# A ReLU-and-sum kernel: two row blocks of 111 and 17 rows per partition in place of three of 1, 111 and 16

## The chip, the cores and the metric

The kernel runs on one core of a Trainium2 chip. A core has several engines that work at the same time and wait for one another through semaphores. Three of them matter here: VectorE (DVE in the profile), ScalarE (ACT) and SyncE (SP), which in this kernel only issues DMAs. The data lie in the chip's HBM; DMA engines bring them into the on-chip memory, SBUF, which has 128 partitions. The metric is the time of one execution on the device in microseconds (us), given as a median of several runs.

## The reference

```
batch, seq, dim = 32, 512, 1024
x: float32 [32, 512, 1024]
relu_x = np.maximum(x, 0)
return np.sum(relu_x, axis=-1).astype(np.float32)      # [32, 512]
```

There are 16,384 rows of 1024 values. Of each row the negative values are set to zero and the rest is summed. The input has 67.1 MB and the output 64 KB.

## The kernel before, in words

**Tiling.** Each of the 128 partitions works on 128 rows. The rows of x are cut into three regions (`REGIONS = [1, 111, 16]`, the rows per partition). In a region of n rows per partition, partition p holds the n neighbouring rows from p * n on. So region 0 is one contiguous run of 128 rows; in region 1 the rows of neighbouring partitions are 111 rows (444 KB) apart, and in region 2 they are 16 rows (64 KB) apart. `res` holds the 128 sums of each partition, one column per row, in the order in which the rows come in.

**Chunks.** `buf` has three buffers of 16 rows per partition. Seven chunks of 16 rows go round them (`CHUNKS`). Chunk 0 is made of two DMAs, one row of region 0 and then 15 rows of region 1; chunks 1 to 6 are 16 rows of region 1 each. Behind them comes the tail, all of region 2, in pieces of 8, 4 and 2 rows (`TAIL`), and then the last two rows in four parts by columns: `first` (columns 0 to 911 of the first of them), `second` (columns 400 to 1023 of the last one), `third` (its columns 224 to 399), and the part across the border of the two rows (the last 112 columns of the one and the first 224 of the other), which goes to a tile of its own, `seam`.

**Who issues what.** All DMAs are issued by SP, in program order. The two of chunk 0 are moved to the very front of the program. Before chunk c (c at least 3) SP waits at line 90 until DVE has finished the reduces of chunk c-3, whose buffer is taken over; the same wait stands before the tail, for chunk 4. The tail's pieces are issued at line 104, the column parts at line 115, the seam at line 118. After that SP waits for a transposed tile and stores it (lines 119 to 122), waits for the end of chunk 6 on both engines and for the landing of `third` (lines 123 to 125), stores the 111 columns of region 1 (line 126), and at the end stores the last region (line 224) once both engines have finished (`s_last`). Lines 225 and 226 wait for the stores to land.

**Who computes what.** For chunks 0 to 5, ACT applies the ReLU in place in steps of several rows (line 154, `ACT_STEPS`), and DVE sums these rows with a reduce (line 169, `DVE_STEPS`); each reduce adds one to `s_dve`. In chunk 5, four rows are left out of the steps and done one by one, two on each engine. Such a single row is one instruction on either engine, ReLU and sum together (`on_act` and `on_dve`, lines 130 and 133), and is followed by a short instruction that reads the accumulator. Chunk 6 is done in this manner by both engines: even rows on DVE, odd rows on ACT (lines 185 to 188). In the tail's pieces the rows are counted from the start of the piece: even offsets go to DVE, odd ones to ACT (lines 193 to 198). The last two rows are shared out by columns (lines 200 to 220), and their part sums are collected in `seam` and summed last.

**The first region's way out.** Region 0 has one sum per partition, in column 0 of `res`. After chunk 1, DVE transposes columns 0 to 31 of `res` in blocks of 32 x 32 (line 178), so that the sums of region 0 lie along four partitions, and SP stores four runs of 128 bytes.

Of the kernel before, what the change touches and what calls it, by code (L numbers as in the profile page):

```python
# [3 lines left out]
P = 128  # L4
D = 1024
BIG = 16
NB = 3
REGIONS = [1, 111, 16]
CHUNKS = [[(0, 0, 1), (1, 0, 15)]] + [[(1, 16 * c + 15, 16)] for c in range(6)]
ACT_STEPS = [[16], [7, 9], [7, 9], [7, 9], [4, 5, 7], [3, 4, 5]]  # L10
DVE_STEPS = [[16], [7, 4, 5], [7, 4, 5], [7, 4, 5], [4, 5, 7], [3, 4, 5]]
TAIL = [8, 4, 2]
CUT = 912
HEAD = 224
MID = 400
# [3 lines left out]
def bass_relu_sum_kernel(  # L19
# [14 lines left out]
    fp32 = mybir.dt.float32  # L34
# [4 lines left out]
    B, S, _ = x.shape  # L39
    J = B * S // P  # L40
    NBIG = len(CHUNKS)
    assert BIG * NBIG + sum(TAIL) + 2 == J == sum(REGIONS)

    xr = x.rearrange("b s d -> (b s) d")
    of = out.rearrange("b s -> (b s)")
    start = [sum(REGIONS[:i]) for i in range(len(REGIONS))]
    xv = [
        xr[P * s : P * (s + n), :].rearrange("(p j) d -> p j d", p=P)
        for s, n in zip(start, REGIONS)
    ]  # L50
    ov = [of[P * s : P * (s + n)].rearrange("(p j) -> p j", p=P) for s, n in zip(start, REGIONS)]

    buf = nc.alloc_sbuf_tensor("buf", [P, NB, BIG, D], fp32)
    w = D - CUT
    seam = nc.alloc_sbuf_tensor("seam", [P, 2 + w + HEAD + 3], fp32)
    res = nc.alloc_sbuf_tensor("res", [P, J], fp32)
    turned = nc.alloc_sbuf_tensor("turned", [P, 32], fp32)
    aside = nc.alloc_psum_tensor("aside", [P, 4 * D], fp32)

    n_in = NBIG + len(TAIL) + 3  # L60
    s_in = [nc.alloc_semaphore(f"s_in{i}") for i in range(n_in)]
    s_act = nc.alloc_semaphore("s_act")
    s_dve = nc.alloc_semaphore("s_dve")
    s_fact = nc.alloc_semaphore("s_fact")
    s_fdve = nc.alloc_semaphore("s_fdve")
    s_half = nc.alloc_semaphore("s_half")
    s_seam = nc.alloc_semaphore("s_seam")
    s_last = nc.alloc_semaphore("s_last")
    s_turn = nc.alloc_semaphore("s_turn")
    s_store = nc.alloc_semaphore("s_store")  # L70
    s_out = nc.alloc_semaphore("s_out")

    sp, act, dve = nc.sync, nc.scalar, nc.vector

    NTWO = len(ACT_STEPS)
    done = [sum(map(len, DVE_STEPS[: c + 1])) for c in range(NTWO)]


    tb = NBIG % NB


    code = nc.main_func.blocks[0].instructions
# [5 lines left out]
    for c in range(NBIG + 1):  # L88
        if c >= NB:
            sp.wait_ge(s_dve, done[c - NB])  # L90
        if c < NBIG:
            i = 0
            for g, j, n in CHUNKS[c]:
                sp.dma_start(  # L94
                    out=buf[:, c % NB, i : i + n, :], in_=xv[g][:, j : j + n, :]
# [5 lines left out]
    r = 0  # L101
    tail = []
    for i, n in enumerate(TAIL):
        sp.dma_start(out=buf[:, tb, r : r + n, :], in_=xv[-1][:, r : r + n, :]).then_inc(  # L104
            s_in[NBIG + i], 16
        )
        tail.append((r, n, s_in[NBIG + i]))
        r += n


    rows = xv[-1].rearrange("p j d -> p (j d)")[:, r * D : (r + 2) * D]
    flat = buf[:, tb, r : r + 2, :].rearrange("p j d -> p (j d)")
    first, second, third = [(0, CUT), (D + MID, 2 * D), (D + HEAD, D + MID)]
    for k, (lo, hi) in enumerate((first, second, third)):
        sp.dma_start(out=flat[:, lo:hi], in_=rows[:, lo:hi]).then_inc(  # L115
            s_in[NBIG + len(TAIL) + k], 16
        )
    sp.dma_start(out=seam[:, 2 : 2 + w + HEAD], in_=rows[:, CUT : D + HEAD]).then_inc(s_seam, 16)
    sp.wait_ge(s_turn, 1)
    sp.dma_start(  # L120
        out=of[0:P].rearrange("(k q) -> k q", q=32), in_=turned[0:P:32, 0:32]
    ).then_inc(s_store, 16)
    sp.wait_ge(s_fact, 1)
    sp.wait_ge(s_fdve, 1)
    sp.wait_ge(s_in[-1], 16)
    sp.dma_start(out=ov[1][:, :], in_=res[:, start[1] : start[2]]).then_inc(s_store, 16)


    def on_act(t, acc, to=None):
        return act.activation(t if to is None else to, t, AF.Relu, accum_out=acc)  # L130

    def on_dve(t, acc, to=None):
        return dve.tensor_scalar(  # L133
            out=t if to is None else to,
            in0=t,
            scalar1=0.0,
            scalar2=None,
            op0=ALU.max,
            op1=ALU.add,
            accum_out=acc,  # L140
        )

    def row(c, i):
        return buf[:, c % NB, i, :], res[:, c * BIG + i : c * BIG + i + 1]

    k = 0
    for c in range(NTWO):
        alone = BIG - sum(ACT_STEPS[c])
        act.wait_ge(s_in[c], 16 * len(CHUNKS[c]))
        r = 0  # L150
        ready = []
        for n in ACT_STEPS[c]:
            t = buf[:, c % NB, r : r + n, :]
            act.activation(t, t, AF.Relu).then_inc(s_act, 1)  # L154
            k += 1
            ready += [k] * n
            r += n
        for i in range(BIG - alone // 2, BIG):
            on_act(*row(c, i))
        if alone:  # L160
            dve.wait_ge(s_in[c], 16 * len(CHUNKS[c]))
            for i in range(BIG - alone, BIG - alone // 2):
                on_dve(*row(c, i))
        r = seen = 0
        for n in DVE_STEPS[c]:
            if ready[r + n - 1] > seen:
                seen = ready[r + n - 1]
                dve.wait_ge(s_act, seen)
            dve.tensor_reduce(  # L169
                out=res[:, c * BIG + r : c * BIG + r + n],  # L170
                in_=buf[:, c % NB, r : r + n, :],
                axis=X,
                op=ALU.add,
            ).then_inc(s_dve, 1)
            r += n
        if c == 1:
            dve.wait_ge(s_dve, done[c])
            dve.transpose(out=turned[:, :], in_=res[:, 0:32]).then_inc(s_turn, 1)  # L178


    j0 = NBIG * BIG
    for c in range(NTWO, NBIG):
        act.wait_ge(s_in[c], 16 * len(CHUNKS[c]))
        dve.wait_ge(s_in[c], 16 * len(CHUNKS[c]))
        for i in range(BIG):
            ins = (on_act if i % 2 else on_dve)(*row(c, i))
            if i >= BIG - 2:
                ins.then_inc(s_fact if i % 2 else s_fdve, 1)
    aside_rows = [aside[:, i * D : (i + 1) * D] for i in range(1, 4)]
    for r, n, s in tail:  # L190
        act.wait_ge(s, 16)
        dve.wait_ge(s, 16)
        for i in range(r, r + n):
            t, acc = buf[:, tb, i, :], res[:, j0 + i : j0 + i + 1]
            if (i - r) % 2:
                on_act(t, acc, aside_rows.pop(0) if i >= sum(TAIL) - 5 else None)
            else:
                on_dve(t, acc)
# [6 lines left out]
    k = 2 + w  # L205
# [18 lines left out]
    sp.dma_start(out=ov[-1][:, :], in_=res[:, start[-1] : J]).then_inc(s_out, 16)  # L224
    sp.wait_ge(s_store, 16 * (len(REGIONS) - 1))
    sp.wait_ge(s_out, 16)
# [28 lines left out]
```

## Time and profile before

| What | Value |
|---|---|
| Median of 3 runs | 160.76 us (160.74 to 160.83) |
| The profiled execution, its own time | 160.78 us |
| Its span | 159.4 us |
| DVE busy | 120.7 us, 76% |
| ACT busy | 101.4 us, 64% |
| DMA queue of SP, share of 16 engines' span | 98.0% |
| HBM read, mean rate over the span | 67.11 MB, 421 GB/s |
| One row of 1024 columns on DVE (line 133) | 1216 ns |
| One row of 1024 columns on ACT (line 130, into `buf`) | 1042 ns |
| Reduce of 16 rows on DVE (line 169) | 17221 ns |
| Reduce of 7 rows on DVE (line 169) | 7602 ns |
| Transpose on DVE (line 178) | 213 ns |

The span runs from the first to the last instruction that the hardware profiler saw; the execution's own time is 1.4 us longer. "Busy" counts the instructions of an engine without its waits. A wait is listed as idle time before the instruction that it held up, with an arrow to what ended it. "SPq" is the queue in which SP issues its DMAs; the time to landing counts from the issue until the semaphore is complete. Durations of neighbouring instructions on one engine overlap a little, since the next one starts while the last one drains.

### The profile page before, as it was taken

Reading aid. Unit: us, or ns where it says so; the run is one execution under the profiler, and the core shown is the slowest. Engines: PE = TensorE matmul, PEld = TensorE weight load, DVE = VectorE, ACT = ScalarE, POOL = GpSimd, SP = SyncE. Lnnn points to the kernel's source line nnn. Section 1 sums busy time; section 2 is a strip of 40 time slices with the busy share of each in tenths; the row PEclk is TensorE's granted clock in tenths of the full one; section 3 lists DMA queues with packets and bytes.
Section 4 is the critical chain, followed back from the end, with each engine's and each line's share of the span. In section 5 each row is a group of like instructions: output and inputs, shape, how many; then the busy total and the mean of one; then the engine's idle time right before and its main releaser. Section 6 shows DMA issues by size and latency. Waiting matters only on the chain.

```text
span 159.4 us, 150 instructions
## 1 busy us (share of the span) xinstructions
DVE 120.7 (76%) x59; ACT 101.4 (64%) x54; POOL 0.2 (0%) x4
## 2 busy tenths in 40 slices
DVE  0000000009999999999999999999999999898995
ACT  3000059990799808996099951999329990496975
POOL 0000000000000000000000000000000000000000
DMA  9997996996997998989969969969969979798994
GB/s 378 493 401 339 493 526 263 526 526 263 526 460 329 526 411 378 526 362 428 526 296 493 526 263 526 526 263 526 510 280 526 444 345 526 304 485 366 423 399 146
DMA packets 2457, 67.18 MB, mean 421 GB/s; under 512 B 536, under 2 KB 792, under 8 KB 1176
## 3 DMA queue, kind: packets, MB, share of 16 engines
q1 hardware_dynamic: 2456, 67.18, 98.0%
q14 instruction: 1, 0.01, 0.0%
HBM read 67.11 MB, written 0.07 MB: 421 GB/s over the span
## 4 chain that ended last, share of the span: by engine, by line
DVE 54%; DMA 34%; ACT 9%; SPq 1%; issue 0%
DVE res L169 54%; DMA buf<-in_x_dram 34%; ACT buf L154 9%; SPq L104 1%; SPq L115 0%; DVE seam L133 0%; SPq L94 0%; ACT aside L130 0%; DVE turned L178 0%
## 5 line engine op out<-in xcount | busy, mean ns | idle before, releaser
L169 DVE TENSOR_REDUCE res<-buf 128x4 f32<-128x4096 f32 (+4 forms) x16 | 99.3, 6276 | 35.6 <-ACT buf L154 35.6
L154 ACT ACTIVATE buf<-buf 128x7168 f32<-128x7168 f32 (+5 forms) x13 | 80.4, 6233 | 46.2 <-DMA buf<-in_x_dram 46.2
L133 DVE TENSOR_SCALAR_CACHE_REDUCE buf<-buf 128x1024 f32<-128x1024 f32 (+3 forms) x20 | 20.9, 1100 | 1.6 <-DMA buf<-in_x_dram 1.4
L130 ACT ACTIVATE buf<-buf 128x1024 f32<-128x1024 f32 x14 | 14.6, 1042 | 7.9 <-DMA buf<-in_x_dram 7.9
L130 ACT ACTIVATE aside<-buf 128x1024 f32<-128x1024 f32 (+2 forms) x5 | 4.1, 828 | 1.1 <-DMA buf<-in_x_dram 1.0
L130 ACT ACTIVATION_READ_ACCUMULATOR buf<-buf 128x1 f32 x14 | 2.6, 186 | 0.0
L154 ACT ACT_TABLE_LOAD x1 | 1.3, 1283 | 1.3 <-PEq L240 1.3
L133 DVE DVE_READ_ACCUMULATOR buf<-buf 128x1 f32 x20 | 1.7, 83 | 0.0
L130 ACT ACTIVATION_READ_ACCUMULATOR aside<-buf 128x1 f32 x5 | 0.9, 187 | 0.0
L133 DVE TENSOR_SCALAR_CACHE_REDUCE seam<-seam 128x227 f32<-128x227 f32 x1 | 0.4, 391 | 0.0
L130 ACT ACTIVATE aside<-seam 128x114 f32<-128x114 f32 x1 | 0.3, 270 | 0.0
L178 DVE STREAM_TRANSPOSE turned<-res 128x32 f32<-128x32 f32 x1 | 0.2, 213 | 0.0
L130 ACT ACTIVATION_READ_ACCUMULATOR aside<-seam 128x1 f32 x1 | 0.2, 186 | 0.0
L240 POOL MEMSET const-bfloat16-1.0<- 128x1 bf16 x1 | 0.1, 102 | 0.0
L240 POOL MEMSET const-uint8-127<- 128x1 uint8 x1 | 0.1, 102 | 0.0
L240 POOL MEMSET const-float32-1.0<- 128x1 f32 x1 | 0.1, 99 | 0.0
L240 POOL MEMSET const-float32-0.0<- 128x1 f32 x1 | 0.1, 98 | 0.2 <-issue 0.2
L133 DVE DVE_READ_ACCUMULATOR seam<-seam 128x1 f32 x1 | 0.1, 82 | 0.0
## 6 DMA issues: line engine op xcount, KB each, us to landing
buf<-in_x_dram SPq DMA_DIRECT2D x1, 7680.0 KB, 21.2
buf<-in_x_dram SPq DMA_DIRECT2D x1, 4096.0 KB, 25.5
buf<-in_x_dram SPq DMA_DIRECT2D x1, 2048.0 KB, 30.0
buf<-in_x_dram SPq DMA_DIRECT2D x1, 1024.0 KB, 32.0
buf<-in_x_dram SPq DMA_DIRECT2D x1, 512.0 KB, 3.4
buf<-in_x_dram SPq DMA_DIRECT2D x1, 456.0 KB, 32.6
buf<-in_x_dram SPq DMA_DIRECT2D x1, 312.0 KB, 33.0
seam<-in_x_dram SPq DMA_DIRECT2D x1, 168.0 KB, 32.6
```

The lines of the kernel that those rows point to most:

```text
L104: sp.dma_start(out=buf[:, tb, r : r + n, :], in_=xv[-1][:, r : r + n, :]).then_inc(s_in[NBIG + i], 16)
L130: return act.activation(t if to is None else to, t, AF.Relu, accum_out=acc)
L133: return dve.tensor_scalar(out=t if to is None else to, in0=t, scalar1=0.0, scalar2=None, op0=ALU.max, op1=ALU.add, accum_out=acc,)
L154: act.activation(t, t, AF.Relu).then_inc(s_act, 1)
L169: dve.tensor_reduce(out=res[:, c * BIG + r : c * BIG + r + n], in_=buf[:, c % NB, r : r + n, :], axis=X, op=ALU.add,).then_inc(s_dve, 1)
L178: dve.transpose(out=turned[:, :], in_=res[:, 0:32]).then_inc(s_turn, 1)
L240: nc = _bacc.Bacc("TRN2", target_bir_lowering=False, num_devices=1)
```

## The change

The rows are cut into two regions, of 111 and 17 rows per partition. The first DMA takes one row per partition of the first region, at the region's stride, and the second DMA its next 15 rows; the chunks 1 to 5 are 16 rows and chunk 6 is 15 rows. The tail is the second region: 9, 4 and 2 rows and the last two by columns. It starts in the row of the buffer that chunk 6 leaves free and runs on into the next buffer, through a view `line` of the buffers as one run of rows. Chunk 0 is reduced in two steps, of 7 and 9 rows. In chunk 6, ACT takes the even rows and DVE the odd ones. The transpose, its tile, its semaphore and its store are gone; the first region's store takes columns 0 to 110 of `res`, and the last store has 17 columns.

```
-REGIONS = [1, 111, 16]
-CHUNKS = [[(0, 0, 1), (1, 0, 15)]] + [[(1, 16 * c + 15, 16)] for c in range(6)]
+REGIONS = [111, 17]
+CHUNKS = [[(0, 0, 1), (0, 1, 15)]] + [[(0, 16 * c, 16)] for c in range(1, 6)] + [[(0, 96, 15)]]
 ACT_STEPS = [[16], [7, 9], [7, 9], [7, 9], [4, 5, 7], [3, 4, 5]]
-DVE_STEPS = [[16], [7, 4, 5], [7, 4, 5], [7, 4, 5], [4, 5, 7], [3, 4, 5]]
-TAIL = [8, 4, 2]
+DVE_STEPS = [[7, 9], [7, 4, 5], [7, 4, 5], [7, 4, 5], [4, 5, 7], [3, 4, 5]]
+TAIL = [9, 4, 2]
...
+    j0 = sum(n for c in CHUNKS for _, _, n in c)
...
-    turned = nc.alloc_sbuf_tensor("turned", [P, 32], fp32)
...
-    s_turn = nc.alloc_semaphore("s_turn")
...
-    tb = NBIG % NB
+    line = buf[:, :, :, :].rearrange("p b j d -> p (b j) d")
+    t0 = NBIG % NB * BIG - (BIG - CHUNKS[-1][0][2])
...
     for i, n in enumerate(TAIL):
-        sp.dma_start(out=buf[:, tb, r : r + n, :], in_=xv[-1][:, r : r + n, :]).then_inc(
+        sp.dma_start(out=line[:, t0 + r : t0 + r + n, :], in_=xv[-1][:, r : r + n, :]).then_inc(
             s_in[NBIG + i], 16
         )
...
-    flat = buf[:, tb, r : r + 2, :].rearrange("p j d -> p (j d)")
+    flat = line[:, t0 + r : t0 + r + 2, :].rearrange("p j d -> p (j d)")
...
-    sp.wait_ge(s_turn, 1)
-    sp.dma_start(
-        out=of[0:P].rearrange("(k q) -> k q", q=32), in_=turned[0:P:32, 0:32]
-    ).then_inc(s_store, 16)
     sp.wait_ge(s_fact, 1)
     sp.wait_ge(s_fdve, 1)
     sp.wait_ge(s_in[-1], 16)
-    sp.dma_start(out=ov[1][:, :], in_=res[:, start[1] : start[2]]).then_inc(s_store, 16)
+    sp.dma_start(out=ov[0][:, :], in_=res[:, : start[1]]).then_inc(s_store, 16)
...
-        if c == 1:
-            dve.wait_ge(s_dve, done[c])
-            dve.transpose(out=turned[:, :], in_=res[:, 0:32]).then_inc(s_turn, 1)
-
-    j0 = NBIG * BIG
...
     for c in range(NTWO, NBIG):
+        last = sum(n for _, _, n in CHUNKS[c]) - 1
         act.wait_ge(s_in[c], 16 * len(CHUNKS[c]))
         dve.wait_ge(s_in[c], 16 * len(CHUNKS[c]))
-        for i in range(BIG):
-            ins = (on_act if i % 2 else on_dve)(*row(c, i))
-            if i >= BIG - 2:
-                ins.then_inc(s_fact if i % 2 else s_fdve, 1)
+        for i in range(last + 1):
+            ins = (on_dve if i % 2 else on_act)(*row(c, i))
+            if i >= last - 1:
+                ins.then_inc(s_fdve if i % 2 else s_fact, 1)
...
         for i in range(r, r + n):
-            t, acc = buf[:, tb, i, :], res[:, j0 + i : j0 + i + 1]
+            t, acc = line[:, t0 + i, :], res[:, j0 + i : j0 + i + 1]
             if (i - r) % 2:
                 on_act(t, acc, aside_rows.pop(0) if i >= sum(TAIL) - 5 else None)
             else:
                 on_dve(t, acc)
```

More of the change, by code (lines that the diff above doesn't have):

```diff
@@ L41, in bass_relu_sum_kernel @@
     NBIG = len(CHUNKS)
-    assert BIG * NBIG + sum(TAIL) + 2 == J == sum(REGIONS)
+    j0 = sum(n for c in CHUNKS for _, _, n in c)
+    assert j0 + sum(TAIL) + 2 == J == sum(REGIONS)
     xr = x.rearrange("b s d -> (b s) d")
```

## The prediction, made before the result was known

> **What bounds the kernel now.** I read the page first, for the shares of the engines and of the DMA queue.
>
> ```profile
> span 159.4 us, 150 instructions
> DVE 120.7 (76%) x59; ACT 101.4 (64%) x54; POOL 0.2 (0%) x4
> q1 hardware_dynamic: 2456, 67.18, 98.0%
> ```
>
> The queue that brings x in is busy 98% of the span; VectorE (DVE), busier than ScalarE (ACT), stands at 76%. The kernel is a stream of loads, and the times at which ACT starts each chunk confirm it: chunks 0 to 5 start at 21.70, 41.05, 60.41, 79.76, 99.10 and 118.45 us, every 19.35 us for 16 rows per partition, 1.21 us a row. Before the tail, compute matters only if it holds up an issue on SP. So I went to the end, first in the chain of work that ended last.
>
> ```profile
> 122.04 0.33 SPq L104
> ...
> 123.86 32.98 DMA buf<-in_x_dram
> 156.84 0.02 issue
> 156.86 0.03 ACT aside L130
> 156.88 0.43 issue
> 157.32 0.20 ACT aside L130
> 157.51 0.02 issue
> 157.53 0.40 DVE seam L133 x2
> ```
>
> The tail's loads are issued around 122 to 125 us and land 33 us later: they queue behind chunk 6. After the landing of `second` at 156.86 only 1.1 us of compute is left before the last store. The chain's long run of L169 ahead of this is an issue condition with much slack, not a cost: the tail was issued at 122.04, when the stream still had chunk 6 to move until 137.81.
>
> Third, the order of time from the landing of the tail's first piece (8 rows), for DVE and the store, with the idle time before each instruction in brackets.
>
> ```profile
> 147.53 1.22 DVE L133 TENSOR_SCALAR_CACHE_REDUCE buf<-buf 128x1024 f32<-128x1024 f32 x1 [0.50 <-DMA buf<-in_x_dram]
> ...
> 150.95 1.22 DVE L133 TENSOR_SCALAR_CACHE_REDUCE buf<-buf 128x1024 f32<-128x1024 f32 x1
> ...
> 152.09 0.08 DVE L133 DVE_READ_ACCUMULATOR buf<-buf 128x1 f32 x1
> ...
> 152.42 1.22 DVE L133 TENSOR_SCALAR_CACHE_REDUCE buf<-buf 128x1024 f32<-128x1024 f32 x1 [0.24 <-DMA buf<-in_x_dram]
> ...
> 154.94 1.22 DVE L133 TENSOR_SCALAR_CACHE_REDUCE buf<-buf 128x1024 f32<-128x1024 f32 x1 [0.15 <-DMA buf<-in_x_dram]
> ...
> 156.08 0.62 DVE L133 TENSOR_SCALAR_CACHE_REDUCE buf<-buf 128x456 f32<-128x456 f32 x1
> ...
> 156.86 0.37 DVE L133 TENSOR_SCALAR_CACHE_REDUCE buf<-buf 128x208 f32<-128x208 f32 x1
> ...
> 157.16 0.33 DVE L133 TENSOR_SCALAR_CACHE_REDUCE buf<-buf 128x176 f32<-128x176 f32 x1
> ...
> 157.53 0.39 DVE L133 TENSOR_SCALAR_CACHE_REDUCE seam<-seam 128x227 f32<-128x227 f32 x1
> ...
> 157.96 0.34 SPq L224 DMA_DIRECT2D out_dram<-res  x1
> ```
>
> This list decides the case. DVE does every other row; its starts are 1.14 us apart (150.95 minus 147.53, by 3), since each starts when its predecessor's accumulator read starts. Between the pieces its idle time is only 0.24, 0.15 and, before 156.86, about 0.15 us: some 0.5 us of slack from 147.53 to the end.
>
> **The change part by part.** The profiled execution took 160.78 us for a span of 159.4, and the median of the runs is 160.76. What I add to the span I add to 160.76.
>
> *The tail's first piece, 9 rows for 8.* Chunk 6 is one row shorter, so 120 rows per partition have come in when the piece lands, exactly as before (1+111+8 then, 111+9 now), in as many DMAs: it lands at 147.53 if the start of the stream is unchanged. The tail's loop is untouched and gives DVE the rows with even offset: of 8 rows 4, of 9 rows 5; ACT keeps 4. From 147.53 DVE then has 5+2+1 rows without a gap: 8 x 1.14 = 9.12, to 156.65. The half of `first` (456 columns) takes 0.55 from start to the next accumulator read (156.08 to 156.63): 157.20. That is 0.34 after the landing of `second`, the wait that ended last before. Then 208 columns (0.30, from 156.86 to 157.16): 157.50; 176 columns to its accumulator read (0.25, to 157.41): 157.75; from that read to the seam 0.12 (157.41 to 157.53): 157.87. The seam stood at 157.53. **+0.34 us**. The waits between cost nothing once fulfilled: the one before 156.08 leaves the 1.14 spacing. Behind the late seam stand s_last, SP's last issue (157.96 becomes 158.30) and its store; ACT's last part also waits for DVE's 176 columns and moves as far. The other DMA waits of the tail (4 rows, 2 rows, `first`, `second`, `third`, seam load) are then all over before DVE asks.
>
> *Chunk 6, 15 rows, parity swapped.* It lands one row earlier, at 137.81 - 1.21 = 136.60. ACT takes 8 rows at 1.04 (138.87 to 139.91): 144.9. DVE, still in its reduces until 137.27, takes 7 at 1.14: 145.3. Both are ready for 147.53 with 2.2 us in hand; cost nothing. That slack can't be spent: the ninth row lands with its piece.
>
> *Chunk 0's reduce in two steps (7, 9), the transpose gone.* A 7-row reduce takes 7602 ns and the 16-row one 17221 ns, 1069 ns a row; 7+9 make 17.34, so at most +0.12 on DVE. The transpose and its wait gave the next reduce its start at 70.22 after an end at 70.07: -0.15. SP's issue of chunk 3 moves from 52.84 to at most 52.96, while chunk 2 keeps the queue busy until 60.41; the tail's issue at 122.04 has the same cover until 136.6. Nothing, with over 7 us of slack at each.
>
> *The transposed store.* On SP its 0.64 us issue at 125.34 goes, ahead of a wait that lasts until 157.16; in the rings its 0.5 KB lies behind the seam load. The queue's own waits show whether its landing was ever waited for:
>
> ```profile
> SPq L125 <- DMA buf<-in_x_dram: 31.1, 1, 31.1
> SPq L226 <- DMA out_dram<-res: 1.1, 1, 1.1
> ```
>
> No wait stands at L225 (s_store); only the last store, L226, is waited for. So removing it saves nothing. [...]
>
> *The stores that stay.* The large one keeps 444 bytes per partition and is issued at the landing of `third`, 157.16. The last one has 68 bytes per partition instead of 64. The trace shows packets of the 444-byte store from 158.0 to 158.42 and of the 64-byte one from 158.79 to 159.09: 0.42 and 0.30 us. So 4 bytes more, no longer on 64-byte steps, cost 0 to +0.12; it is far nearer the 64-byte row, and I take **+0.02**.
>
> *The tail's pitch, 17 rows for 16.* Eight rows took 147.53 - 137.81 = 9.72 us against 8 x 1.21 = 9.68 at the stream's pace: 0.04 at most to win, and I take 0. [...]
>
> *The first row, strided.* The first DMA read 512 KB in one run; now it reads 128 pieces of 4 KB, 444 KB apart. No row shows this at the start. Before, it landed 3.4 us after its issue, of which 1.21 are data at the stream's pace. In the DMA records few packets run from about 1.1 to 1.4 us, a hole of 0.3. If the hole goes: -0.3; if another like it comes: +0.3. The floor is the landing of the 8 KB store, 1.4 us, plus 1.21 of data: 2.6 against 3.4, -0.8. The nearest rows are `first`, 128 strided pieces of 3.6 KB, landed 1.1 us behind the 2-row piece against 1.08 by its bytes, and chunk 0's other 15 rows, already 444 KB apart, at 18.25 us against 18.14. They say that stride is harmless, so I take 0. What the start gains or loses goes through whole: it moves 147.53.
>
> Sum: 0.34 + 0.02 = 0.36, **161.12 us**. A measurement of this kernel can tell about 0.2% (0.32 us) from no change, so this lies just past that line.
>
> **The rivals.** *The start is slower:* 0.36 + 0.3 gives 161.42. For it: in the old order the first bytes came from one contiguous run. Against: the 15 strided rows behind lost only 0.1.
>
> *The start is quicker and cancels:* without the hole, 147.53 becomes 147.23 and the end stands at 160.82, within 0.2%. For it: the hole is there. Against: nothing in it points to contiguity.
>
> *Faster:* the start is the only place ahead of 147.53 with time to recover. The first landing must come more than 0.68 us sooner (0.36 to pay back, 0.32 to be seen), at 2.7 after its issue; at the floor of 2.6 the sum is 160.3. Against: all of the latency but 0.1 would have to go.
>
> **How the numbers follow.** DVE's odd row with the start unchanged: 0.62, own range 161.0 to 161.25; the line at 161.08 cuts it, about 0.50 above and 0.12 below. Slower start: 0.12. Quicker start that cancels: 0.17. Faster: 0.09. So slower 0.62, same 0.29, faster 0.09. The range reaches to both start cases, 160.75 to 161.5; what is left out is the faster case and a start that loses more than 0.4.
>
> **What would show it.** Right: five DVE rows from the tail's first landing, no DMA wait on DVE from there to the seam, the seam starting 10.34 us after that landing (10.00 before), and the last issue 0.34 later against it. The landing itself, 147.53 before, reads the start by itself, and the first DMA's 3.4 us says whether the stride did it. Packets of the last store over more than 0.3 us would show the 68 bytes. Wrong: a landing moved by over 0.3, or DVE rows not 1.14 apart.

## The result, and the profile after

The changed kernel takes 161.57 us (median of 6 runs, 161.44 to 162.21); the kernel before, on the same chip, 160.82. The ratio is 1.005, with a 95% interval of 1.0033 to 1.0067: slower, by 0.75 us. The forecast was slower, 161.12, with a range up to 161.5. The direction and one mechanism were right; the size was twice what was forecast, and the time lies 0.07 us above the range.

The profiled execution took 161.55 us for a span of 160.2 (before: 160.78 for 159.4). First the page, its span, its engines and its DMA queue:

```profile
span 160.2 us, 149 instructions
DVE 120.2 (75%) x59; ACT 101.4 (63%) x54; POOL 0.2 (0%) x4
q1 hardware_dynamic: 2448, 67.18, 97.7%
```

The stream is as full as before, and DVE even works half a microsecond less, 0.2 of it the transpose that is gone. None of this says where 0.8 us went. The chain that ended last does (start, duration, what):

```profile
0.42 21.47 DMA buf<-in_x_dram
...
122.10 25.63 DMA buf<-in_x_dram
147.73 0.02 issue
147.75 10.31 DVE buf L129 x22
158.06 0.02 issue
158.09 0.40 DVE seam L129 x2
```

Before, the DMA carried the chain until 156.84. Now it hands over to DVE at 147.75, the landing of the 9-row piece, and DVE carries it to the seam in 22 instructions without a break. In the order of time, from chunk 0 on ACT to the last issue on SP:

```profile
21.92 13.86 ACT L150 ACTIVATE buf<-buf 128x16384 f32<-128x16384 f32 x1 [19.39 <-DMA buf<-in_x_dram]
...
147.75 1.22 DVE L129 TENSOR_SCALAR_CACHE_REDUCE buf<-buf 128x1024 f32<-128x1024 f32 x1 [2.45 <-DMA buf<-in_x_dram]
...
152.32 1.22 DVE L129 TENSOR_SCALAR_CACHE_REDUCE buf<-buf 128x1024 f32<-128x1024 f32 x1
...
156.88 0.62 DVE L129 TENSOR_SCALAR_CACHE_REDUCE buf<-buf 128x456 f32<-128x456 f32 x1
...
157.43 0.36 DVE L129 TENSOR_SCALAR_CACHE_REDUCE buf<-buf 128x208 f32<-128x208 f32 x1
...
158.09 0.39 DVE L129 TENSOR_SCALAR_CACHE_REDUCE seam<-seam 128x227 f32<-128x227 f32 x1
...
158.51 0.34 SPq L217 DMA_DIRECT2D out_dram<-res  x1
```

And from the list of DMA issues, the first load and the last store, with KB and the time from issue to landing:

```profile
buf<-in_x_dram SPq DMA_DIRECT2D x1, 512.0 KB, 3.8
...
out_dram<-res SPq DMA_DIRECT2D x1, 8.5 KB, 1.6
```

Subtract the same moments of the two profiles, and the difference falls into three pieces:

| Stretch | Before | After | Difference |
|---|---|---|---|
| Start to chunk 0 on ACT | 21.70 | 21.92 | +0.22 |
| Chunk 0 to the landing of the tail's first piece | 125.83 | 125.83 | 0 |
| That landing to the seam on DVE | 10.00 | 10.34 | +0.34 |
| Seam to the last issue | 0.43 | 0.42 | 0 |
| Last issue to its landing | 1.4 | 1.6 | +0.2 |

The sum is 0.76, and the profiled executions differ by 0.77. The first DMA landed 3.8 us after its issue instead of 3.4.

### The profile page after: what moved, and what is told of

The parts are those of the page before. It is cut to its first block, busy times and chain, and to the rows that moved or that the text cites. A ratio compares the mean times of both kernels' runs of the same rounds, so it can differ in the third digit from the quotient of the medians.

```text
span 160.2 us, 149 instructions
## 1 busy us (share of the span) xinstructions
DVE 120.2 (75%) x59; ACT 101.4 (63%) x54; POOL 0.2 (0%) x4
## 4 chain that ended last, share of the span: by engine, by line
DVE 61%; DMA 29%; ACT 9%; SPq 0%; issue 0%
DVE res L165 54%; DMA buf<-in_x_dram 29%; ACT buf L150 9%; DVE buf L129 6%; DVE seam L129 0%; SPq L94 0%
## 5 line engine op out<-in xcount | busy, mean ns | idle before, releaser
L165 DVE TENSOR_REDUCE res<-buf 128x7 f32<-128x7168 f32 (+4 forms) x17 | 99.3, 5915 | 35.8 <-ACT buf L150 35.8
```

The costliest lines, as they stand in the source:

```text
L165: dve.tensor_reduce(out=res[:, c * BIG + r : c * BIG + r + n], in_=buf[:, c % NB, r : r + n, :], axis=X, op=ALU.add,).then_inc(s_dve, 1)
```

## The experiments

The theory that the table gives is three separate losses: the strided first read, DVE's fifth row, and the 68-byte store. "Excess" below is a kernel's median less that of the kernel before on the same chip (160.83, 160.82 and 160.81 in the three groups). The changed kernel's excess is 0.75.

### DVE's fifth row

```
-            if (i - r) % 2:
+            if (i - r) % 2 != n % 2:
```

> The changed kernel with one edit: in the tail's 9-row piece ACT takes the even offsets (5 rows) and DVE the odd ones (4). Theory (three separate losses: +0.22 us at the start, +0.34 us from DVE's fifth row, +0.2 us at the last store): the seam starts 10.00 us after the landing of the first tail piece instead of 10.34, DVE waits for DMAs again in the tail, and the time falls by 0.34, to about 161.2. Rival (the tail's end is set by something else, the 17-row pitch of the small loads or SP): the seam stays 10.3 us behind that landing and the time stays at 161.55.

Measured: 161.67 us, excess 0.84, no gain at all. Yet DVE's fifth row was undone, as the profile of this run shows in the order of time:

```profile
147.88 1.22 DVE L129 TENSOR_SCALAR_CACHE_REDUCE buf<-buf 128x1024 f32<-128x1024 f32 x1 [2.46 <-DMA buf<-in_x_dram]
...
157.91 0.39 DVE L129 TENSOR_SCALAR_CACHE_REDUCE seam<-seam 128x227 f32<-128x227 f32 x1
...
158.33 0.34 SPq L217 DMA_DIRECT2D out_dram<-res  x1
```

The seam starts 10.03 us after the landing. Most of this gain of 0.31 is lost outside the span: an execution's own time less its span is 1.36 us in the mean for the changed kernel and 1.35 for the kernel before, but 1.61 here. The rest is not accounted for; in this profile chunk 0 also starts 0.13 us later than in the changed kernel's (22.05 against 21.92). One thing in the page goes with it. The changed kernel's page, like that of the kernel before, lists under the DMA queues one transfer of instructions (0.01 MB) inside the span, about 1.4 us after the last store's issue; this run's page has none.

So the next run swapped the parity of chunk 6 as well, which gives each engine back its number of instructions:

```
-            ins = (on_dve if i % 2 else on_act)(*row(c, i))
+            ins = (on_act if i % 2 else on_dve)(*row(c, i))
             if i >= last - 1:
-                ins.then_inc(s_fdve if i % 2 else s_fact, 1)
+                ins.then_inc(s_fact if i % 2 else s_fdve, 1)
...
-            if (i - r) % 2:
+            if (i - r) % 2 != n % 2:
```

> The changed kernel with the parity of the 9-row piece swapped as in the run that did only that (ACT 5 rows, DVE 4), and the parity of chunk 6 swapped too (DVE 8 rows, ACT 7), so that each engine has as many instructions as in the changed kernel. Theory (the first parity run did shorten the span, but one instruction more on ACT or one less on DVE moved a transfer of instructions behind the end of the span and cost 0.26 us there): seam 10.0 us after the landing of the first tail piece, time outside the span back at 1.35 us from 1.61, time 161.2 (0.34 below the changed kernel). Rival (the time outside the span grows because of the earlier end itself, or of the parity of the piece): outside stays at 1.6 and the time at 161.6.

Measured: 161.22 us, excess 0.40, so 0.35 less than the changed kernel; 1.36 us outside the span. The transfer is back in the page's list of queues, and the seam stands 10.01 us behind the landing:

```profile
q1 hardware_dynamic: 2448, 67.18, 97.8%
q14 instruction: 1, 0.01, 0.0%
```

```profile
147.81 1.22 DVE L129 TENSOR_SCALAR_CACHE_REDUCE buf<-buf 128x1024 f32<-128x1024 f32 x1 [1.29 <-DMA buf<-in_x_dram]
...
157.82 0.39 DVE L129 TENSOR_SCALAR_CACHE_REDUCE seam<-seam 128x227 f32<-128x227 f32 x1
```

DVE's fifth row costs 0.35 us. That the first attempt lost its gain to the number of instructions was then put to the kernel before, where moving a row from DVE to ACT changes nothing on the path:

```
-            ins = (on_act if i % 2 else on_dve)(*row(c, i))
+            ins = (on_act if i % 2 or i == 0 else on_dve)(*row(c, i))
```

> The kernel before with one row of chunk 6 (its first) moved from DVE to ACT; both engines then still finish before the tail's first piece lands, so nothing on the path moves. Theory (the number of instructions on an engine decides where the instruction transfer falls): span unchanged at 159.5, time outside the span 1.61 instead of 1.35, time 161.1; no instruction transfer inside the span. Rival (the time outside the span hangs on something else in the parity kernels): 160.83 with 1.35 outside.

Measured: 161.00 us, excess 0.18 (ratio 1.0012, 1.0003 to 1.002), with a mean span of 159.42 against 159.47 and 1.59 us outside instead of 1.37. That is what the theory expected outside the span. Which of the two engines matters was asked with one reduce less on DVE and ACT untouched:

```
-DVE_STEPS = [[16], [7, 4, 5], [7, 4, 5], [7, 4, 5], [4, 5, 7], [3, 4, 5]]
+DVE_STEPS = [[16], [7, 9], [7, 4, 5], [7, 4, 5], [4, 5, 7], [3, 4, 5]]
```

> The kernel before with chunk 1 reduced in two steps (7, 9) instead of three (7, 4, 5): one instruction less on DVE, none more on ACT, nothing on the path. If the number on DVE moves the transfer of instructions: 1.6 us outside the span and 161.05. If it is the number on ACT: 1.36 outside and 160.83.

Measured: 161.29 us, excess 0.48 (ratio 1.0027, 1.0017 to 1.0038), mean span 159.40 and 1.87 us outside. Its page's list of queues, again without instructions:

```profile
q1 hardware_dynamic: 2456, 67.18, 98.1%
HBM read 67.11 MB, written 0.07 MB: 421 GB/s over the span
```

Removing an instruction that was nowhere near the path made the kernel 0.3% slower. The number on DVE is enough to do it; whether ACT's does something too was not tried alone, and why this edit costs 0.50 outside the span and the other 0.22 stays open.

The traces hold DMA records behind the end of the span too, and they show where the transfers went. The digits are the busy share of the DMA engines from 159.3 to 161.3 us, 0.05 us each: first in the kernel before (span 159.4 us), then in this run (159.4), then in the run with 112 and 16 rows further down (159.7).

```profile
DMA  8000000000000000000000000000000000000000
```

```profile
DMA  0000000000000000000000000000600000040000
```

```profile
DMA  0000000006000000000000000000000000000000
```

In the kernel before, one transfer starts 0.1 us ahead of the end of the span. In this run there are two, 1.3 and 1.7 us behind it. The other three runs with more time outside the span (the first parity run, the row moved to ACT, and the run with three edits below) also have two, 1.3 to 1.4 us behind it. The run with 112 and 16 rows has one, 0.1 us behind the end; so its page lists none either, yet its time outside the span is the usual 1.35. A page without the transfer is therefore no sign of the loss; two late transfers are, in the four runs that have them. All ten profiles without the loss count 59 instructions on DVE, these four count 57 or 58.

### The first read

```
-                    out=buf[:, c % NB, i : i + n, :], in_=xv[g][:, j : j + n, :]
+                    out=buf[:, c % NB, i : i + n, :],
+                    in_=xr[0:P, :].rearrange("(p j) d -> p j d", p=P) if c + i == 0 else xv[g][:, j : j + n, :],
```

> The changed kernel with one edit: the first DMA reads the first 128 rows of x as one contiguous run, as before the change, instead of 128 rows that lie 444 KB apart; the sums of that one row per partition are then those of other rows. Theory (the stride of the first read costs the start 0.22 us): the first DMA lands 3.4 us after its issue instead of 3.8, chunk 0 starts on ACT at 21.70 instead of 21.92, the tail's first piece lands at 147.53, and the time falls by 0.22, to about 161.33. Rival (the start differs for another reason, such as the removed store or the layout of the other chunks): chunk 0 stays at 21.9 and the time does not move.

Measured: 161.42 us, excess 0.59. The first load landed 3.3 us after its issue, and chunk 0 started 0.05 us before it does in the kernel before. From the order of time:

```profile
21.65 13.86 ACT L151 ACTIVATE buf<-buf 128x16384 f32<-128x16384 f32 x1 [19.10 <-DMA buf<-in_x_dram]
...
147.52 1.06 ACT L127 ACTIVATE buf<-buf 128x1024 f32<-128x1024 f32 x1 [2.49 <-DMA buf<-in_x_dram]
```

By the medians the gain is 0.16, a little less than in the trace. The opposite edit was made in the kernel before, once with the pitch of 444 KB and once with one of 64 KB:

```
-CHUNKS = [[(0, 0, 1), (1, 0, 15)]] + [[(1, 16 * c + 15, 16)] for c in range(6)]
+CHUNKS = [[(1, 110, 1), (1, 0, 15)]] + [[(1, 16 * c + 15, 16)] for c in range(6)]
```

> The kernel before with one edit: its first DMA reads the last row of each partition's 111 (128 rows that lie 444 KB apart) instead of 128 contiguous rows; the sums stored for the first region are then those of other rows. Theory (the stride of the first read costs the start 0.25 us by itself, whatever the rest of the kernel): first DMA lands at 3.6 to 3.9 us, chunk 0 starts on ACT at 21.9, time 161.08. Rival (it is the two neighbouring reads of the same 444 KB blocks, or the other layout of the changed kernel): chunk 0 at 21.7, time 160.83.

Measured: 160.99 us, excess 0.17 (ratio 1.0008, 0.9999 to 1.0016), first landing 3.6 us, chunk 0 at 21.77. The size agrees with the other direction (0.16), though this interval alone just reaches no change.

```
-CHUNKS = [[(0, 0, 1), (1, 0, 15)]] + [[(1, 16 * c + 15, 16)] for c in range(6)]
+CHUNKS = [[(2, 0, 1), (1, 0, 15)]] + [[(1, 16 * c + 15, 16)] for c in range(6)]
```

> The kernel before with its first DMA reading the first row of each partition's 16 in the last region (128 rows that lie 64 KB apart) instead of 128 contiguous rows; the sums stored for the first region are then those of other rows. Theory A (any read that is not contiguous starts slower): 160.98 as with 444 KB, first landing 3.6. Theory B (the reach of the read counts, 8 MB here against 57): about 160.85, first landing 3.4.

Measured: 161.14 us, excess 0.33 (ratio 1.002, 1.0011 to 1.0028). Both theories missed: the shorter pitch is not cheaper than the long one, and the time is 0.16 above what theory A gave. From this run's list of issues and its order of time:

```profile
buf<-in_x_dram SPq DMA_DIRECT2D x1, 512.0 KB, 3.9
```

```profile
22.02 13.86 ACT L154 ACTIVATE buf<-buf 128x16384 f32<-128x16384 f32 x1 [19.47 <-DMA buf<-in_x_dram]
```

So here a first read that isn't contiguous does start the stream later, and a shorter reach did not make it cheaper (excess 0.33 us at 64 KB, 0.17 at 444 KB). Over all profiles the two kinds do not overlap. Six have a contiguous first read: it lands after 3.2 to 3.4 us, and chunk 0 starts at 21.63 to 21.71. Eight have a strided one: 3.6 to 3.9 us, and 21.77 to 22.05. From 0 to 2 us the DMA moves 106 to 133 GB/s in three of the first kind (the kernel before, this section's first run and the run with four edits below) and 55 to 76 in seven of the second (all but the run with both parities swapped). Busy times, DMA share and GB/s from 1 to 2 us, before and after the change:

```profile
1.00:2.00 1.00, 0.00 (x0) 0.73 (x1) 0.00 (x0) 1.00 0.88 250
```

```profile
1.00:2.00 1.00, 0.00 (x0) 0.75 (x1) 0.00 (x0) 1.00 0.99 147
```

The last number of each line is GB/s. So the loss shows already in the first packets of the read itself. No run tells 64 KB from 444 KB: the landing of 3.9 us also occurs at 444 KB, and the two intervals overlap. Why the strided packets start slowly stays open.

### The last store

```
-    sp.dma_start(out=ov[-1][:, :], in_=res[:, start[-1] : J]).then_inc(s_out, 16)
+    sp.dma_start(
+        out=of[P * 112 : P * 128].rearrange("(p j) -> p j", p=P), in_=res[:, 112:J]
+    ).then_inc(s_out, 16)
```

> The changed kernel with one edit: the last store writes 16 columns, 64 bytes per partition on a pitch of 64 bytes, instead of 17 columns on a pitch of 68; one column of sums is not stored, and the others lie elsewhere than they should. Theory (the 68-byte store lands 0.2 us later than the 64-byte one): landing 1.4 us after the issue instead of 1.6, time down by 0.2 to about 161.35. Rival (the landing varies with the order of the stores at the end, or by chance): landing stays at 1.6 and the time does not move.

Measured: 161.28 us, excess 0.45: a gain of 0.30, more than the 0.2 of the profile. The last line of its issues:

```profile
out_dram<-res SPq DMA_DIRECT2D x1, 8.0 KB, 1.4
```

Size and place had changed together there. The next run kept the 64 bytes per partition and put them back on the pitch of 68:

```
-    sp.dma_start(out=ov[-1][:, :], in_=res[:, start[-1] : J]).then_inc(s_out, 16)
+    sp.dma_start(out=ov[-1][:, 1:], in_=res[:, start[-1] + 1 : J]).then_inc(s_out, 16)
```

> The changed kernel with a last store of 16 columns, 64 bytes per partition, left on the 68-byte pitch of the output (the first column of the second region is not stored). Theory A (it is the 64-byte grid that counts: runs that start and end off it land later): landing stays at 1.6 to 1.7 us, time 161.55. Theory B (it is the size, more than 64 bytes in one run): landing 1.4 us and time 161.3, as in the run with 64 bytes on a 64-byte pitch.

Measured: 161.49 us, excess 0.67; nearly all of the gain is gone with the size unchanged. Its profile has, for this store,

```profile
out_dram<-res SPq DMA_DIRECT2D x1, 8.0 KB, 2.0
```

which is the longest of its five runs (161.88); at the median the landing should be nearer 1.6, an estimate from 161.88 less 161.49. In all nine profiles with the 64-byte pitch the last store lands after 1.4 us, and in the five with the pitch of 68 after 1.6 to 2.0. So it is the grid and not the 4 bytes, as far as one run of five executions shows it; the intervals of the two runs overlap (1.0017 to 1.0037 and 1.0025 to 1.0053). Where in the store the time goes is seen in the DMA records of a window of 0.6 us from the first packets on, cut into 40 slices. First the run with 64 bytes on a 64-byte pitch, from 159.18 us, then the run with 64 bytes on the pitch of 68, from 159.26:

```profile
DMA  0003667655643310000000000000000000900000
```

```profile
DMA  0003667655543310000000000000000000000000
```

The packets run for the same 0.2 us, from 0.8 us after the issue (158.38 and 158.46) in both. The rest, 0.4 us to the landing in the one and 1.0 in the other, passes with no packet of the store under way. (The lone 9 is the transfer of instructions.) Why it is longer on the pitch of 68 was not shown.

### All together, and the other way to cut

The first three edits in one kernel, and later the same with chunk 6's parity swapped too (their diffs are those shown above):

> The changed kernel with all three edits: ACT takes five of the nine rows, the first DMA reads a contiguous run, the last store writes 64 bytes per partition at 64-byte pitch (the sums of one row per partition are those of other rows and one column is not stored). Theory (the three losses are separate and are all of the difference): they add up, 0.22 + 0.34 + 0.2, and the time is that of the kernel before, 160.8, within 0.1. Rival (the losses hide one another or a fourth is there): it stays 0.2 or more above the kernel before, or falls below it.

Measured: 161.23 us, excess 0.40, with a mean span of 159.59 and 1.62 us outside it. The span is within 0.1 of the kernel before (159.51), and the rest is the 0.26 outside; DVE has 57 instructions here, as in the first parity run.

> The changed kernel with ACT on five of the nine rows, chunk 6 with DVE on the even rows (so each engine keeps its number of instructions), a contiguous first read and a last store of 64 bytes on a 64-byte pitch (one row's sums per partition are those of other rows, one column is not stored). Theory (start 0.17, DVE's fifth row 0.34, store 0.29, and the 0.25 of the run with three edits was the instruction count): all of the difference is gone, 160.83 within 0.1, with 1.36 outside the span. Rival (a fourth loss in the changed layout): 0.2 or more above the kernel before.

Measured: 161.03 us, excess 0.22; ratio 1.0007, 0.9998 to 1.0016. The trace of its profiled run equals that of the kernel before moment by moment: chunk 0 at 21.68, the tail's first landing at 147.51, the seam at 157.55, the last issue at 157.97, landing 1.4; and the mean outside is back at 1.36. But the profiled run (160.81) is the quickest of the eleven. The medians leave 0.22, which is in the rival's terms (0.2 or more), and the interval includes none. If there is a fourth loss it is under 0.26 us; these runs don't decide it.

```
-REGIONS = [111, 17]
-CHUNKS = [[(0, 0, 1), (0, 1, 15)]] + [[(0, 16 * c, 16)] for c in range(1, 6)] + [[(0, 96, 15)]]
+REGIONS = [112, 16]
+CHUNKS = [[(0, 0, 1), (0, 1, 15)]] + [[(0, 16 * c, 16)] for c in range(1, 7)]
...
-TAIL = [9, 4, 2]
+TAIL = [8, 4, 2]
```

> Two regions of 112 and 16 rows per partition, chunks of 16 rows, tail pieces of 8, 4 and 2 rows: no transposed store, as in the changed kernel, but a tail of 16 rows as before. Theory (two of the three losses come from the odd 17th row): DVE has four rows in the first tail piece and the last store 64 bytes on a 64-byte pitch, so only the strided first read is left, 160.83 + 0.17 = 161.0. Rival (losses come from having two regions as such): 161.3 or more.

Measured: 161.04 us, excess 0.23 (ratio 1.0012, 1.0003 to 1.0021). In the order of time:

```profile
147.76 1.22 DVE L129 TENSOR_SCALAR_CACHE_REDUCE buf<-buf 128x1024 f32<-128x1024 f32 x1 [0.50 <-DMA buf<-in_x_dram]
...
157.78 0.39 DVE L129 TENSOR_SCALAR_CACHE_REDUCE seam<-seam 128x227 f32<-128x227 f32 x1
...
158.21 0.34 SPq L217 DMA_DIRECT2D out_dram<-res  x1
```

The whole output is stored, nothing is transposed, and two of the three losses are gone: they come from the seventeenth row, not from having two regions. What is left is the start (147.76 against 147.53). No run beats the kernel before.

## Why the prediction was right or wrong, point by point

*The tail's first piece:* right in size and in mechanism. Forecast +0.34 between that landing and the seam, 10.34 us; the profile has 10.34, with no DMA wait on DVE in between, and the run that gave the row to ACT and kept the number of instructions took 0.35 off. One remark beside the sum was off: "some 0.5 us of slack" adds the idle times in brackets. What a further row can use runs from the accumulator read behind which the next row could start. Two of the three such reads, before the change:

```profile
154.70 0.08 DVE L133 DVE_READ_ACCUMULATOR buf<-buf 128x1 f32 x1
...
156.63 0.08 DVE L133 DVE_READ_ACCUMULATOR buf<-buf 128x1 f32 x1
```

The gaps are 0.33 (152.09 to 152.42), 0.24 (to 154.94) and 0.23 (to 156.86), together 0.80, and a row of 1.14 less 0.80 is the 0.34.

*Chunk 6, chunk 0's reduce, the transposed store:* costed at nothing, and nothing shows on the path. DVE is ready 2.45 us ahead of the 9-row piece (2.2 were forecast), and the stretch from chunk 0 to that landing is 125.83 us in both kernels. That no wait stood at the removed store's semaphore was the right thing to read. But one part of the reasoning was luck: instructions off the path were taken as free. DVE lost its transpose and gained a reduce, which left it at 59 instructions and the time outside the span at 1.36 us; one fewer cost the kernel before 0.50 us there, more than any term in the sum.

*The tail's pitch:* 0 forecast, and 0 is what the unchanged 125.83 says.

*The first row, strided:* this step failed. "They say that stride is harmless, so I take 0": it measured +0.22 in the profile and 0.16 to 0.17 by the runs in both directions. The rows chosen as nearest, the tail's small pieces and chunk 0's other 15 rows, run behind others in a full queue (they landed 21.2 to 33.0 us after their issue, before the change); none of them has to start a stream. The strided read falls behind from 1 to 2 us already: 147 GB/s instead of 250. The rival with the slower start (+0.3) described what happened, with a chance of 0.12.

*The stores that stay:* this step failed as well. +0.02 was taken and 0 to +0.12 allowed; +0.2 was in the profile and 0.30 in the run that undid it. The bound was made from the wrong row: the time in which the packets run. Its two readings were too long besides. Here are the packets of the 444-byte store, from 157.9 to 158.7 us in 40 slices, and those of the 64-byte store, from 158.7 to 159.4, both before the change:

```profile
DMA  0000035577977997653110000000000000000000
```

```profile
DMA  0000015684565321000000000000000000900000
```

They run from 158.00 to 158.32 and from 158.79 to 159.00 us, so for 0.32 and 0.21 us and not 0.42 and 0.30; the bound stays at 0.11. The packets of the last store take about the same 0.2 us before and after, so the sign named for this loss, packets over more than 0.3 us, did not come though the loss did: the extra comes after the last packet. The row that could have warned was the 1.4 us of the old store, of which its packets cover only a small part; nothing was known of the remainder, and it needed an upper end of its own.

With the two steps at their measured sizes the sum is 0.34 + 0.22 + 0.2 = 0.76 us, 161.52, against 161.57 measured. By the runs that undid each they are 0.35 + 0.16 + 0.30 = 0.81, against 0.75. Each of the two alone lay near or inside what the range allowed for; both at once put the time 0.07 above it.

## What to carry to other kernels

When an odd row is given to a pipeline whose last pieces are shared out by parity, count the rows of each engine from the last landing on: here one row of 1.14 us ate 0.80 us of slack and showed 0.34. Price a small store at the very end from issue to landing, not from its packets; here the packets took about 0.2 us and the landing 1.4 on a 64-byte pitch, 1.6 to 2.0 on a pitch of 68. Price the first load by a load that starts a stream, not by one in a full queue; here its stride cost 0.16 to 0.22 us. When an edit gains in the span but not in the execution's own time, look at what lies outside the span before doubting the mechanism.

## What the runs showed of the hardware that was not expected

Three things. A last store of 64 bytes per partition on a 64-byte pitch lands after 1.4 us; one of 64 or 68 bytes on a pitch of 68 after 1.6 to 2.0, with packets that run equally long. A first load of 128 pieces of 4 KB lands 3.2 to 3.4 us after its issue when contiguous, and 3.6 to 3.9 when it is strided, whether at 444 KB or at 64 KB.

And the number of instructions on DVE goes with the time outside the span: 1.35 to 1.38 us in the mean with 59 of them, 1.59 to 1.62 with 57, 1.87 with 58. With 57 or 58, two transfers of instructions start 1.3 us or more behind the end of the span; with 59, one starts between 0.7 us ahead of it and 0.1 us behind it. One reduce fewer on DVE went with 0.50 us. What sets the time of these transfers was not shown. That the late transfers are what costs the time is inferred from the two going together; no run separates them.
